# A transformer block on one core: the order of the first requests, and eight row slots in the head

## The chip, the cores and the metric

The kernel runs on 1 core of one Trainium2 chip. The metric is the device time of one execution in microseconds (us). TensorE multiplies, VectorE (DVE), ScalarE (ACT) and GpSimd (POOL) do the elementwise work, and SyncE (SP) issues nearly all transfers between HBM and SBUF. Each engine takes its instructions in the order in which they were written for it and waits on semaphores.

## What is computed

The reference is one transformer block in float32, on x of 1024 rows by 1024 columns:

```python
for l in range(DEPTH):                                   # DEPTH = 1
    x = x + _hybrid_mixer(_rms_norm(x, norm1_g[l]), w_in[l], ...)
    x = x + _memory_xattn(_rms_norm(x, norm2_g[l]), mem, ...)
    x = x + _sq_relu_mlp(_rms_norm(x, norm3_g[l]), w_ff_in[l], w_ff_out[l])
```

The mixer begins with one projection, whose columns are split into the inputs of two attention branches (a top-k one, and one with compressed, selected and windowed keys):

```python
proj = h @ w_in
c_q, c_kv, k_idx, w_idx, q_nsa, kv_nsa, g_nsa = jnp.split(proj, splits, axis=-1)
```

The change touches only how this projection starts: `_rms_norm(x, norm1_g)`, and the product of the first 512 rows with columns 968 to 1224 of `w_in`, which hold the keys and values that are compressed in blocks of 32 positions.

## The kernel before

The 1024 rows are eight tiles of 128, in two parts of four (`PARTS`, L27). `project` (L371) does the projection of one part. Part 0 is the **head** of the program and runs alone; part 1 and all later dense work run beside the attention of earlier tiles (`together`, L113), and the last dense work stands at the end.

In the head each tile of x is loaded (L378), squared and summed on ScalarE (L288), scaled by its inverse root and by the gain norm1_g on VectorE (L290), turned by eight transposes on TensorE (L277), and split into a rounded high half xh on ScalarE (L238) and a low half xl, the rest, on VectorE (L239). Weights are loaded in groups of 256 rows (`load_w`, L254) into a ring of four raw slots and split likewise into whi on ScalarE (L247) and wlo on GpSimd or VectorE (L252). A product in `gemm` (L303) loads the four groups of a chunk of columns and then goes over the four tiles; every tile is 8 k-steps of three matmuls (xh by whi, xh by wlo, xl by whi; L221), summed in one PSUM buffer and then consumed (`consume`, L408). The first chunk, columns 968 to 1224, is copied by a relu-tagged tile (L434), transposed (L437) and stored as the compression's input. The chunks that follow use the same four row tiles.

Ahead of all that, the constants are asked for where `build` comes to them: the identity (L226), cos and sin (L349, L350), the q gains (L352 to L354), the xq gain (L358), the masks (L359, L361, through two slots of the row ring and a cast, L204), and the position encodings of the compression (`pe_stack`, L1143), which are transposed on TensorE and copied on GpSimd (L486, L487) to the end of the compression's input. In `project`, after the tiles, come the gains of the compressed queries and keys and a table (L387 to L390), and seven rows of key gains (L397). Most of these are one row sent to all 128 partitions.

Row tiles, the gain norm1_g, the normalized rows and the masks' raw form share one ring of SBUF slots, tag `x4` (L38), five slots in the head.

The order on each engine is not the order of the lines. The program is built with `schedule_with_timeline_sim` (L82): a scheduler sets the order of each engine's instructions from its own model of their times, with the written order as a guide. Every request of SyncE also waits for the landing of the request eight places before it, since eight semaphores are used in turn.

Of the kernel before, what the change touches and what calls it, by code (L numbers as in the profile page):

```python
# [9 lines left out]
F32 = mybir.dt.float32  # L10
# [7 lines left out]
ALU = mybir.AluOpType  # L18
# [4 lines left out]
P = 128  # L23
L = 1024
DM = 1024
NT = L // P
PARTS = ((0, 4), (4, 4))  # L27
# [6 lines left out]
KG = 2  # L34
NS = 4
G = 2
RINGS = {
    "p1": {"x4": 5, "st": 2, "relu": 4, "wraw": 4, "whi": 6, "wlo": 6, "c8": 4, "c4": 2, "kraw": 5, "pc": 2},  # L38
    "p2": {"x4": 3, "st": 1, "relu": 2, "whi": 4, "wlo": 4, "c8": 3, "c4": 1, "kraw": 4, "pc": 2},
    "dn": {"b4": 4, "h": 8, "relu": 2, "wraw": 2, "whi": 4, "wlo": 4},  # L40
    "res": {"b4": 4},
# [45 lines left out]
def drain(gen):  # L87
    for _ in gen:
        pass
# [80 lines left out]
def build(nc, tc, I, C, out):  # L170
    v, s, g, te = nc.vector, nc.scalar, nc.gpsimd, nc.tensor
    ctx = ExitStack()
    W = {n: I[n][0] for n in I}
# [14 lines left out]
    def ring(pool, tag, shape, dt=F32):  # L188
        n = RINGS[pool.name if isinstance(pool.name, str) else "dn"][tag]
        return pool.tile(shape, dt, tag=tag, name=tag, bufs=n)  # L190

    def row(ap):
        return ap[None, :]

    def const(name, shape, pool=cst):
        t = pool.tile(shape, F32, tag=name, name=name)
        nc.sync.dma_start(t, C[name])
        return t

    def const16(name, shape):  # L200
        t = at.tile(shape, BF16, tag=name, name=name)
        f = ring(p1, "x4", shape)
        nc.sync.dma_start(f, C[name])
        v.tensor_copy(t, f)  # L204
        return t

    def bcast(name, src, w):
        t = cst.tile([P, w], F32, tag=name, name=name)
        nc.sync.dma_start(t, src.to_broadcast([P, w]))
        return t  # L210

    def swap(x):
        return halves(x)[..., ::-1, :]

    def halves(x):
        if len(x.shape) == 2:
            return x.rearrange("p (j i) -> p j i", j=2)
        return x.rearrange("p h (j i) -> p h j i", j=2)

    def mm(o, a, b, start, stop):  # L220
        te.matmul(o, a, b, start=start, stop=stop)  # L221

    def small(pool, tag, w, dt=F32, bufs=2, p=P):
        return pool.tile([p, w], dt, tag=tag, name=tag, bufs=bufs)

    ident = const("c_ident", [P, P])  # L226
    mhalf = cst.tile([P, 1], F32, tag="mhalf", name="mhalf")
    v.memset(mhalf, -0.5)
# [25 lines left out]
    def load_w(pool, shape, *srcs):  # L254
        raw = ring(pool, "wraw", shape)
        for dst, src in srcs:
            nc.sync.dma_start(dst(raw), src)
        hi, lo = ring(pool, "whi", shape, F32R), ring(pool, "wlo", shape, F32R)
        split_w(raw, hi, lo)
        return hi, lo  # L260
# [3 lines left out]
    def load_whole(pool, shape, *srcs):  # L264
        wholes["i"] += 1
        raw = ring(pool, ("whi", "wlo")[wholes["i"] % 2], shape)
        for dst, src in srcs:
            nc.sync.dma_start(dst(raw), src)
        return [raw]
# [30 lines left out]
            v.scalar_tensor_tensor(xn, x_t[:, c:c + 512], r[:, 0:1], gb[c // 512], op0=ALU.mult, op1=ALU.mult)  # L300
            to_T(pool, xn, [x[:, c // P:c // P + 4] for x in xs], 4)

    def gemm(pool, xs, nk, nt, wsrc, chunks, consume):  # L303

        for ci, parts in enumerate(chunks):
            w = sum(n for _, n in parts)
            gr = []
            for k0 in range(0, nk, KG):
                kn = min(KG, nk - k0)
                srcs, o = [], 0  # L310
                for c0, n in parts:
                    srcs.append((lambda r, o=o, n=n: r[:, :, o:o + n],
                                 wsrc[k0 * P:(k0 + kn) * P, c0:c0 + n].rearrange("(k p) n -> p k n", p=P)))
                    o += n
                ws = load_w(pool, [P, kn, w], *srcs) if len(xs) == 2 else load_whole(pool, [P, kn, w], *srcs)
                gr += [[x[:, k, :] for x in ws] for k in range(kn)]
            for t in range(nt):
                pt = pst(TAGS[pool.name][0], [P, w])
                for k in range(nk):
                    if len(xs) == 1:  # L320
                        mm(pt, xs[0](t, k), gr[k][0], k == 0, k == nk - 1)
                        continue
                    wh, wl = gr[k]
                    xh, xl = xs[0](t, k), xs[1](t, k)
                    mm(pt, xh, wh, k == 0, False)
                    mm(pt, xh, wl, False, False)
                    mm(pt, xl, wh, False, k == nk - 1)
                consume(ci, t, pt)
                yield nk * (5 - len(xs)) * w / 2400.0

    def xT(pool, nt, whole=False):

        parts = [pool.tile([P, DM // P, nt * P], F32 if whole else F32R, tag="x" + n, name="x" + n)
                 for n in ("h" if whole else "hl")]
        return (parts, [lambda t, k, x=x: x[:, k, t * P:(t + 1) * P] for x in parts],
                lambda t: [x[:, :, t * P:(t + 1) * P] for x in parts])
# [9 lines left out]
            nc.sync.dma_start(gb, row(src[i * 512:(i + 1) * 512]).to_broadcast([P, 512]))  # L346
        return gs

    cos = const("c_cos", [P, NT, 32], at)  # L349
    sin = const("c_sin", [P, NT, 64], at)  # L350
    qg = at.tile([P, 3, 64], F32, tag="qg", name="qg")
    nc.sync.dma_start(qg[:, 0, :], row(W["dsa_qn_g"]).to_broadcast([P, 64]))  # L352
    nc.sync.dma_start(qg[:, 1, :], row(W["nsa_qn_g"]).to_broadcast([P, 64]))
    nc.sync.dma_start(qg[:, 2, :], W["nsa_kn_g"][0:1].to_broadcast([P, 64]))  # L354
    v.tensor_scalar(qg[:, 0:2, :], qg[:, 0:2, :], -1.0, None, op0=ALU.mult)
    qgs = at.tile([P, 3, 64], F32, tag="qgs", name="qgs")
    v.tensor_copy(halves(qgs), swap(qg))
    xqg = bcast("xqg", row(W["xq_norm_g"]), 128)  # L358
    masks = const16("c_masks", [P, 640])  # L359
    window, causal = masks[:, 0:512], masks[:, 128:640]  # L360
    cmask = const16("c_cmask", [P, NT, 64])  # L361
    qraw = [[[dr.tile([P, n, 256], F32, tag=f"q{k}{t}{c}", name=f"q{k}{t}{c}") for c in range(2)] for t, n in PARTS]
            for k in range(3)]
    oT_dr = [[dr.tile([P, P], F32, tag=f"o{t}{c}", name=f"o{t}{c}") for c in range(8)] for t in range(NT)]
# [3 lines left out]
    xo_dr = [dr.tile([P, 512], F32, tag=f"xo{t}", name=f"xo{t}") for t in range(NT)]  # L368


    def project(pool, part, pe, st):  # L371
        t0, nt = PARTS[part]
        gb1 = gain(pool, W["norm1_g"])
        whole = part > 0
        _, xf, xt_of = xT(pool, nt, whole)
        for t in range(nt):
            x_t = ring(pool, "x4", [P, DM])
            nc.sync.dma_start(x_t, I["x"][0, (t0 + t) * P:(t0 + t + 1) * P, :])  # L378
            norm_T(pool, x_t, gb1, xt_of(t))
            yield 1.0  # L380
        cq = [ring(pool, "c8", [P, nt, 2, P], F32 if whole else F32R) for _ in xf]
        ckv = [ring(pool, "c4", [P, nt, P], F32 if whole else F32R) for _ in xf]
        kraw = [ring(pool, "kraw", [P, 6, 64]) for t in range(nt)]
        KT = []
        pc = ring(pool, "pc", [P, 512])
# [59 lines left out]
                s.activation(kraw[t][:, 2 * b:2 * b + 2, :], pt[:, :128].rearrange("p (a d) -> p a d", d=64), AF.Copy)  # L445
                split_ps(pt[:, 128:256].rearrange("p (a d) -> p a d", d=64), V[:, T, :, 0, :], V[:, T, :, 1, :])

        def w_in(chunks, first):
            return gemm(pool, xf, DM // P, nt, W["w_in"], chunks,
                        lambda ci, t, pt: consume(ci + first, t, pt))  # L450

        def consume_kv(ci, t, pt):
            s.activation(kraw[t][:, DSA, :], pt[:, :64], AF.Copy)
# [30 lines left out]
        for kv in range(0 if part else 2):  # L484
            p3 = pe[:, kv, :].rearrange("p (a l) -> p a l", a=2)
            g.tensor_copy(KT[kv][0:64, :, nt * P:], p3[0:64])  # L486
            g.tensor_copy(KT[kv][64:128, :, nt * P:nt * P + 15], p3[64:128, :, 1:])  # L487
        yield from w_in([[(968, 256)]], 4)
        yield from w_in([[(0, 256)], [(256, 200), (1736, 24)]], 0)
        pair_ = (w_in([[(1224, 256)], [(1480, 256)]], 5), compress(pool, part, KT, pe, st, ctab))  # L490
        yield from (alternate if part == 0 else chain)(*pair_)
# [3 lines left out]
        for k, name in ((0, "w_dsa_uq"), (2, "w_idx_q")):  # L495
            yield from gemm(pool, [lambda t, k, c=c: c[:, t, k, :] for c in cq], 2, nt,
                            W[name], [[(0, 256)], [(256, 256)]],
                            lambda ci, t, pt, k=k: stage_q(k, ci, t, pt))
# [644 lines left out]
    def pe_stack():  # L1143
        pe = p1.tile([P, 2, 32], F32, tag="pe", name="pe")
        pe2 = ring(p1, "relu", [P, 2, 2, 64])
        for j in range(2):
            nc.sync.dma_start(pe2[0:32, :, j, :], W["nsa_cmp_pe"].rearrange("k l d -> l k d"))
        pp = pst("M", [P, 2, 32])
        for kv in range(2):
            te.transpose(pp[:, kv, :], pe2[0:32, kv, :, :].rearrange("p a d -> p (a d)"), ident[0:32, 0:32])  # L1150
        s.activation(pe, pp, AF.Copy)
        return pe
# [13 lines left out]
    }  # L1166
    for kv in range(2):
        v.memset(st["cT"][kv], 0.0)
    pe = pe_stack()
    plan["w"] = PLAN_HEAD  # L1170
    drain(project(p1, 0, pe, st))
    plan["w"] = PLAN_MAIN
    p1_psum.__exit__(None, None, None)
    p1_pool.__exit__(None, None, None)
# [6 lines left out]
    def fill():  # L1181
        for part in range(1, len(PARTS)):
            with tc.tile_pool(name="p2", bufs=1, reuse_waits="tile") as p2:
                yield from project(p2, part, pe, st)
            projected.append(part)
        dn = dn_pool.__enter__()
        yield from memory(dn)
        yield 1, PACES[1]
        yield from between(dn, 0, 2, {}, False)
        yield 3, PACES[2]  # L1190
        x2s = {}
        yield from between(dn, 2, 2, x2s, True)
        yield 3, PACES[3]
        yield from mlp(dn, 0, 4, x2s)
        yield 5, PACES[4]
        yield from between(dn, 4, 2, {}, False)
# [40 lines left out]
```

## Time and profile before

| what | value |
|---|---|
| time, median of 3 runs | 1802.85 us (1801.54 to 1806.27) |
| time of the profiled execution | 1801.64 us |
| its span in the profile | 1799.6 us |
| mean granted TensorE clock | 0.977 of full |
| DMA moved over the span | 193.80 MB, mean 108 GB/s |

A line of the order in time gives the start and the length in us, the engine, the line of the kernel, the operation, the tile written and the tile read, the shape and how many were merged; the brackets hold the idle time of that engine before it and what ended it. "SPq" is SyncE's issue of a transfer, not its landing; the landing shows as the end of a wait. In the view of stretches each engine has its busy time and, in parentheses, the number of instructions; the last three numbers are the granted clock, the busy share of the DMA engines, and GB/s.

### The profile page before, as it was taken

The page shows a single profiled execution, that of the slowest core. Times are in us where ns is not written, and L with a number is a line of the kernel's source. Part 1 is how long each engine was busy: PE and PEld are TensorE (multiplying, and loading weights), DVE is VectorE, ACT ScalarE, POOL GpSimd, SP SyncE. Part 2 cuts the span into 40 slices and gives each one's busy share as a digit, 9 for nine tenths or more (in the row PEclk, how much of TensorE's full clock was granted, in tenths as well). Part 3 has the DMA queues.
Part 4 walks back from the last instruction along what each step waited for, and adds up shares of the span by engine and source line. Part 5 has one row for each costly group of instructions (what it writes and reads, how often), then busy time and mean ns, then how long its engine had stood idle before and what let it go on. Part 6 is the DMA issues. An engine that isn't in the chain of part 4 may idle for free.

```text
span 1799.6 us, 28055 instructions
## 1 busy us (share of the span) xinstructions
PE 1696.2 (94%) x9326; PEld 1457.3 (81%) x9326; DVE 951.0 (53%) x2381; ACT 1080.4 (60%) x2703; POOL 892.6 (50%) x1025
## 2 busy tenths in 40 slices
PE   5987999899989999999998999999999889999998
PEld 5986888688878777788886888887988878888887
DVE  4555757665873776365654555646524552222223
ACT  4444659797688579856896557994412543333333
POOL 2356647463551355568576576662211444444445
PEclk9997999999999999999999999999989899999999
DMA  6235221366336321222222122225375642333333
GB/s 193 74 119 150 71 76 58 109 197 177 99 107 192 98 63 42 70 71 79 61 67 83 55 71 67 67 75 187 108 245 158 209 118 84 96 94 98 96 118 107
DMA packets 176977, 193.80 MB, mean 108 GB/s; under 512 B 25664, under 2 KB 144192, under 8 KB 176832
## 3 DMA queue, kind: packets, MB, share of 16 engines
q1 hardware_dynamic: 168896, 181.52, 33.2%
q0 software_dynamic: 7936, 10.49, 2.2%
q8 instruction: 74, 1.21, 0.3%
q14 instruction: 71, 0.58, 0.1%
HBM read 170.98 MB, written 20.97 MB: 107 GB/s over the span
## 4 chain that ended last, share of the span: by engine, by line
PE 67%; DVE 9%; POOL 7%; ACT 5%; issue 5%; DMA 5%; SPq 1%; POOLq 0%; ACTq 0%; DVEq 0%
PE psD L221 48%; PE psS L221 8%; PE psPV L221 5%; PE psPT L698 4%; POOL wlo L252 3%; DMA wraw<-in_w_ff_in_dram 1%; PE psM L277 1%; ACT dmask L639 1%; DVE pl L239 1%; DVE S L681 1%; PE psPT L585 1%; ACT S L683 1%; ACT ph L238 1%; DMA qin<-q 1%; ACT whi L247 1%
## 5 line engine op out<-in xcount | busy, mean ns | idle before, releaser
L252 POOL TENSOR_TENSOR wlo<-wraw,whi 128x512 fp32r<-128x512 f32 (+1 forms) x225 | 309.5, 1380 | 266.7 <-ACT whi L247 263.0
L221 PE MATMUL psD<-whi,h 128*128 128x512 f32 x1024 | 340.7, 401 | 9.7 <-DVE b L1126 5.4
L247 ACT ACTIVATE whi<-wraw 128x512 fp32r<-128x512 f32 x321 | 200.7, 628 | 216.7 <-PE psD L221 156.4
L221 PEld LDWEIGHTS psD<-whi,h 128*128 128x128 f32 x1024 | 193.0, 190 | 55.2 <-DVE b L1126 8.8
L221 PE MATMUL psD<-xh,whi 128*128 128x512 f32 (+1 forms) x576 | 212.1, 372 | 1.2 <-ACT xh L238 0.8
L221 PE MATMUL psD<-xh,wlo 128*128 128x512 f32 (+1 forms) x576 | 212.9, 370 | 0.2 <-POOL wlo L252 0.2
L221 PE MATMUL psD<-xl,whi 128*128 128x512 f32 (+1 forms) x576 | 212.1, 370 | 0.0
L221 PE MATMUL psD<-wlo,h 128*128 128x512 f32 x512 | 203.2, 399 | 1.1 <-POOL wlo L252 1.1
L221 PE MATMUL psD<-whi,xh 128*128 128x256 f32 (+1 forms) x704 | 191.7, 353 | 4.3 <-ACT whi L247 3.2
L221 PE MATMUL psD<-wlo,xh 128*128 128x256 f32 (+1 forms) x704 | 191.3, 354 | 1.3 <-DMA wlo<-in_w_in_dram 0.7
L239 DVE TENSOR_TENSOR pl<-psPT,ph 128x512 fp32r<-128x512 f32 (+1 forms) x232 | 142.0, 620 | 80.1 <-ACT ph L238 77.4
L683 ACT ACTIVATE S<-S,mn 128x128 f32<-128x128 f32 (+7 forms) x192 | 142.6, 744 | 38.5 <-DVE mn L681 36.9
L688 POOL TENSOR_SCALAR S<-S,sums,gi 128x640 f32<-128x640 f32 (+7 forms) x128 | 107.0, 846 | 113.7 <-DVE sums L686 101.8
L252 DVE TENSOR_TENSOR wlo<-wraw,whi 128x512 fp32r<-128x512 f32 (+1 forms) x96 | 83.8, 873 | 148.8 <-ACT whi L247 148.5
L238 ACT ACTIVATE ph<-psPT 128x512 fp32r<-128x512 f32 (+1 forms) x232 | 122.7, 539 | 63.2 <-PE psPT L698 59.0
L221 PEld LDWEIGHTS psD<-wlo,xh 128*128 128x128 f32 x704 | 133.3, 194 | 13.4 <-ACT relu L416 1.2
L221 PEld LDWEIGHTS psD<-whi,xh 128*128 128x128 f32 x704 | 130.7, 194 | 14.2 <-ACT whi L247 3.6
L698 PE MATMUL psPT<-c_ident,S 128*128 128x128 f32 x816 | 131.4, 277 | 3.0 <-POOL S L688 1.6
L221 PEld LDWEIGHTS psD<-xh,whi 128*128 128x128 f32 x576 | 108.8, 189 | 19.3 <-ACT xh L238 1.6
L221 PEld LDWEIGHTS psD<-xh,wlo 128*128 128x128 f32 x576 | 109.0, 189 | 17.6 <-POOL wlo L252 0.9
L221 PEld LDWEIGHTS psD<-xl,whi 128*128 128x128 f32 x576 | 108.8, 189 | 17.1
L221 PE MATMUL psS<-K,qh 128*128 128x384 f32 (+3 forms) x288 | 112.7, 395 | 8.6 <-DVE mn L681 4.0
(282 smaller groups left out, 3863.7 us busy)
## 6 DMA issues: line engine op xcount, KB each, us to landing
wraw<-in_w_ff_in_dram SPq DMA_DIRECT2D x40, 512.0 KB, 4.0
wraw<-in_w_ff_out_dram SPq DMA_DIRECT2D x40, 512.0 KB, 3.9
wraw<-in_w_ff_in_dram SPq DMA_DIRECT2D x64, 256.0 KB, 2.7
wraw<-in_w_ff_out_dram SPq DMA_DIRECT2D x64, 256.0 KB, 2.7
whi<-in_w_out_dram SPq DMA_DIRECT2D x32, 256.0 KB, 3.6
wlo<-in_w_out_dram SPq DMA_DIRECT2D x32, 256.0 KB, 3.7
wraw<-in_w_in_dram SPq DMA_DIRECT2D x24, 256.0 KB, 3.7
q<-st SPq DMA_DIRECT2D x12, 512.0 KB, 2.6
```

Of the source, the lines that this page charges most:

```text
L221: te.matmul(o, a, b, start=start, stop=stop)
L238: s.activation(hi, src, AF.Copy)
L239: v.tensor_tensor(lo, src, hi, op=ALU.subtract)
L247: s.activation(hi, raw, AF.Copy)
L252: (v if l == "v" else g).tensor_tensor(lo, raw, hi, op=ALU.subtract)
L277: te.transpose(pt[:, j, :], x_t[:, (c + j) * P:(c + j + 1) * P], ident)
L585: te.transpose(p2[:, h, :], qd[:, h, :, :].rearrange("p b d -> p (b d)"), ident)
L639: s.activation(mask, src, AF.Sign, bias=c, accum_out=over)
L681: v.tensor_tensor_reduce(out=dst, in0=sp, in1=m, scale=1.0, scalar=mn[:, 0:1] if i else 3e38, op0=ALU.add, op1=ALU.min, accum_out=low)
L683: s.activation(S, S, AF.Exp, bias=low, scale=-1.0, accum_out=sums[:, hh:hh + 1])
L688: g.tensor_scalar(Ss[hh], Ss[hh], sums[:, hh:hh + 1], 1.0 if gate is None else gate[:, hh:hh + 1], op0=ALU.mult, op1=ALU.mult)
L698: te.transpose(p2[:, j, hh, :], S[:, (c + j) * P:(c + j + 1) * P], ident)
```

## The change

The ring `x4` of the head has eight slots in place of five. The first tile of x is asked for ahead of the identity. `project` for part 0 now asks, in this order, for the gain and then alternately for a weight group of the first chunk and a tile of x, before any tile is normalized; `gemm`'s loading of weights becomes a generator, `weights`, from which the first product takes its four groups as `begun`. After the four norms of part 0, all the constants except the identity are asked for, and the position encodings are stacked; then the rest of `project` runs. The values computed are the same.

In the built program SyncE's first ten requests are x, identity, gain, weights, x, weights, x, weights, x, weights. The 21 that follow are cos, sin, three q gains, the xq gain, the position encodings (two), the gains of the compressed queries and keys, the two halves of the table, one key gain, the two masks, and six more rows of key gains. Then come the second chunk's weights. Before, the same 31 requests stand ahead of those weights.

```diff
-    "p1": {"x4": 5, "st": 2, ...
+    "p1": {"x4": 8, "st": 2, ...
...
+    late = {"x": ring(p1, "x4", [P, DM])}
+    nc.sync.dma_start(late["x"], I["x"][0, 0:P, :])
     ident = const("c_ident", [P, P])
...
+    def weights(pool, xs, nk, wsrc, parts):
+        w = sum(n for _, n in parts)
+        for k0 in range(0, nk, KG):
...
+            ws = load_w(pool, [P, kn, w], *srcs) if len(xs) == 2 else load_whole(pool, [P, kn, w], *srcs)
+            for k in range(kn):
+                yield [x[:, k, :] for x in ws]
+
-    def gemm(pool, xs, nk, nt, wsrc, chunks, consume):
+    def gemm(pool, xs, nk, nt, wsrc, chunks, consume, begun=None):
...
+            gr = begun if ci == 0 and begun else list(weights(pool, xs, nk, wsrc, parts))
...
+    ahead = {0: late["x"]}
+    def project(pool, part, late, st):
         gb1 = gain(pool, W["norm1_g"])
...
+        begun = []
+        if not whole:
+            ws = weights(pool, xf, DM // P, W["w_in"], [(968, 256)])
+            for t in range(1, nt):
+                begun += [next(ws) for _ in range(KG)]
+                ahead[t] = ring(pool, "x4", [P, DM])
+                nc.sync.dma_start(ahead[t], I["x"][0, t * P:(t + 1) * P, :])
+            begun += list(ws)
         for t in range(nt):
-            x_t = ring(pool, "x4", [P, DM])
-            nc.sync.dma_start(x_t, I["x"][0, (t0 + t) * P:(t0 + t + 1) * P, :])
+            x_t = ahead.pop(t0 + t, None)
+            if x_t is None:
+                x_t = ring(pool, "x4", [P, DM])
+                nc.sync.dma_start(x_t, I["x"][0, (t0 + t) * P:(t0 + t + 1) * P, :])
             norm_T(pool, x_t, gb1, xt_of(t))
             yield 1.0
+        pe = late["pe"]
...
-    pe = pe_stack()
     plan["w"] = PLAN_HEAD
-    drain(project(p1, 0, pe, st))
+    head = project(p1, 0, late, st)
+    for _ in range(PARTS[0][1]):
+        next(head)
+    cos = const("c_cos", [P, NT, 32], at)
+    sin = const("c_sin", [P, NT, 64], at)
...
+    masks = const16("c_masks", [P, 640])
+    window, causal = masks[:, 0:512], masks[:, 128:640]
+    cmask = const16("c_cmask", [P, NT, 64])
+    late["pe"] = pe_stack()
+    drain(head)
```

More of the change, by code (lines that the diff above doesn't have):

```diff
@@ L37 @@
 RINGS = {
-    "p1": {"x4": 5, "st": 2, "relu": 4, "wraw": 4, "whi": 6, "wlo": 6, "c8": 4, "c4": 2, "kraw": 5, "pc": 2},
+    "p1": {"x4": 8, "st": 2, "relu": 4, "wraw": 4, "whi": 6, "wlo": 6, "c8": 4, "c4": 2, "kraw": 5, "pc": 2},
     "p2": {"x4": 3, "st": 1, "relu": 2, "whi": 4, "wlo": 4, "c8": 3, "c4": 1, "kraw": 4, "pc": 2},
@@ L301, in norm_T2 @@
             to_T(pool, xn, [x[:, c // P:c // P + 4] for x in xs], 4)
-    def gemm(pool, xs, nk, nt, wsrc, chunks, consume):
+    def weights(pool, xs, nk, wsrc, parts):
+        w = sum(n for _, n in parts)
+        for k0 in range(0, nk, KG):
+            kn = min(KG, nk - k0)
+            srcs, o = [], 0
+            for c0, n in parts:
+                srcs.append((lambda r, o=o, n=n: r[:, :, o:o + n],
+                             wsrc[k0 * P:(k0 + kn) * P, c0:c0 + n].rearrange("(k p) n -> p k n", p=P)))
+                o += n
+            ws = load_w(pool, [P, kn, w], *srcs) if len(xs) == 2 else load_whole(pool, [P, kn, w], *srcs)
+            for k in range(kn):
+                yield [x[:, k, :] for x in ws]
+    def gemm(pool, xs, nk, nt, wsrc, chunks, consume, begun=None):
         for ci, parts in enumerate(chunks):
             w = sum(n for _, n in parts)
[L307 to L316, printed above, removed]
+            gr = begun if ci == 0 and begun else list(weights(pool, xs, nk, wsrc, parts))
             for t in range(nt):
@@ L347, in gain2 @@
         return gs
[L349 to L361, printed above, removed]
     qraw = [[[dr.tile([P, n, 256], F32, tag=f"q{k}{t}{c}", name=f"q{k}{t}{c}") for c in range(2)] for t, n in PARTS]
@@ L368, in build @@
     xo_dr = [dr.tile([P, 512], F32, tag=f"xo{t}", name=f"xo{t}") for t in range(NT)]
-    def project(pool, part, pe, st):
+    ahead = {0: late["x"]}
+    def project(pool, part, late, st):
         t0, nt = PARTS[part]
@@ L446, in consume, with w_in @@
                 split_ps(pt[:, 128:256].rearrange("p (a d) -> p a d", d=64), V[:, T, :, 0, :], V[:, T, :, 1, :])
-        def w_in(chunks, first):
+        def w_in(chunks, first, begun=None):
             return gemm(pool, xf, DM // P, nt, W["w_in"], chunks,
-                        lambda ci, t, pt: consume(ci + first, t, pt))
+                        lambda ci, t, pt: consume(ci + first, t, pt), begun)
         def consume_kv(ci, t, pt):
@@ L487, in project @@
             g.tensor_copy(KT[kv][64:128, :, nt * P:nt * P + 15], p3[64:128, :, 1:])
-        yield from w_in([[(968, 256)]], 4)
+        yield from w_in([[(968, 256)]], 4, begun)
         yield from w_in([[(0, 256)], [(256, 200), (1736, 24)]], 0)
@@ L1168, in build @@
         v.memset(st["cT"][kv], 0.0)
-    pe = pe_stack()
     plan["w"] = PLAN_HEAD
-    drain(project(p1, 0, pe, st))
+    head = project(p1, 0, late, st)
[3 more added lines that the diff above has]
+    sin = const("c_sin", [P, NT, 64], at)
+    qg = at.tile([P, 3, 64], F32, tag="qg", name="qg")
+    nc.sync.dma_start(qg[:, 0, :], row(W["dsa_qn_g"]).to_broadcast([P, 64]))
+    nc.sync.dma_start(qg[:, 1, :], row(W["nsa_qn_g"]).to_broadcast([P, 64]))
+    nc.sync.dma_start(qg[:, 2, :], W["nsa_kn_g"][0:1].to_broadcast([P, 64]))
+    v.tensor_scalar(qg[:, 0:2, :], qg[:, 0:2, :], -1.0, None, op0=ALU.mult)
+    qgs = at.tile([P, 3, 64], F32, tag="qgs", name="qgs")
+    v.tensor_copy(halves(qgs), swap(qg))
+    xqg = bcast("xqg", row(W["xq_norm_g"]), 128)
+    masks = const16("c_masks", [P, 640])
[3 more added lines that the diff above has]
+    drain(head)
     plan["w"] = PLAN_MAIN
@@ L1183, in fill @@
             with tc.tile_pool(name="p2", bufs=1, reuse_waits="tile") as p2:
-                yield from project(p2, part, pe, st)
+                yield from project(p2, part, late, st)
             projected.append(part)
```

## The prediction

> **What bounds the kernel now.** I read the page first, for the share of each engine and the chain that ended last; then busy time in stretches, to find where TensorE is not busy; then the order in time of the first 41 us, and the DMA issues of that stretch.
>
> The page of the kernel before, span, engines and the chain by engine:
> ```profile
> span 1799.6 us, 28055 instructions
> PE 1696.2 (94%) x9326; PEld 1457.3 (81%) x9326; DVE 951.0 (53%) x2381; ACT 1080.4 (60%) x2703; POOL 892.6 (50%) x1025
> PE 67%; DVE 9%; POOL 7%; ACT 5%; issue 5%; DMA 5%; SPq 1%; POOLq 0%; ACTq 0%; DVEq 0%
> ```
> TensorE bounds the whole, so a change of the head is worth what it moves TensorE's stream. Busy time in stretches of it:
> ```profile
> 0.00:24.00 24.00, 3.87 (x17) 3.36 (x18) 6.46 (x15) 6.10 (x11) 3.40 (x11) 1.00 0.65 202
> 24.00:41.00 17.00, 16.84 (x131) 16.55 (x130) 13.15 (x19) 12.83 (x26) 5.89 (x6) 1.00 0.71 185
> 41.00:125.00 84.00, 81.81 (x709) 80.83 (x709) 46.31 (x114) 39.94 (x125) 41.14 (x40) 1.00 0.31 91
> 125.00:150.00 25.00, 12.82 (x73) 11.02 (x71) 5.50 (x16) 7.56 (x17) 6.56 (x9) 0.68 0.66 217
> 200.00:1799.00 1599.00, 1533.05 (x8126) 1303.63 (x8126) 846.51 (x2085) 983.90 (x2417) 803.73 (x900) 0.98 0.35 105
> ```
> The first number after the stretch and its length is TensorE's busy time. In the first 24 us it is idle for 24 - 3.87 = 20.1 us; from 24 to 125 it is busy 98.7 of 101. So the head is a wait, then a full stream, and the wait is what the change can take away. Its steps, in order of time (start, length, engine and line):
> ```profile
> 0.73 0.38 SPq L197 DMA_DIRECT2D c_ident<-in_c_ident_dram  x1
> 4.96 2.23 SPq L1147 DMA_DIRECT2D relu<-in_nsa_cmp_pe_dram  x2
> 7.77 0.35 SPq L378 DMA_DIRECT2D x<-in_x_dram  x1
> 13.83 1.06 ACT L288 ACTIVATE x<-x 128x1024 f32<-128x1024 f32 x1 [1.95 <-DMA x<-in_x_dram]
> 15.97 1.28 DVE L290 SCALAR_TENSOR_TENSOR x<-x,nr,x 128x1024 f32<-128x1024 f32 x1 [0.74 <-POOL nr L234]
> 16.40 1.72 SPq L257 DMA_DIRECT2D wraw<-in_w_in_dram  x2
> 17.31 1.97 PE L277 MATMUL psM<-c_ident,x 128*128 128x128 f32 x8 [5.69 <-DVE x L290]
> 21.80 1.40 ACT L247 ACTIVATE whi<-wraw 128x512 fp32r<-128x512 f32 x2 [0.93 <-DMA wraw<-in_w_in_dram]
> 22.48 0.58 PE L221 MATMUL psD<-whi,xh 128*128 128x256 f32 x1 [3.21 <-ACT whi L247]
> 23.82 4.03 SPq L257 DMA_DIRECT2D wraw<-in_w_in_dram  x3
> 24.42 0.56 PE L221 MATMUL psD<-wlo,xh 128*128 128x256 f32 x1
> 27.34 0.41 PE L221 MATMUL psD<-whi,xh 128*128 128x256 f32 x1
> 27.56 0.41 PE L221 MATMUL psD<-whi,xl 128*128 128x256 f32 x1
> 28.36 0.28 PE L221 MATMUL psD<-wlo,xh 128*128 128x256 f32 x1
> 28.47 0.28 PE L221 MATMUL psD<-whi,xl 128*128 128x256 f32 x1
> 29.06 0.68 DVE L239 TENSOR_TENSOR xl<-psM,xh 128x512 fp32r<-128x512 f32 x1
> 30.13 1.09 ACT L238 ACTIVATE xh<-psM 128x512 fp32r<-128x512 f32 x2 [0.42 <-PE psM L277]
> 40.91 0.60 ACT L434 ACTIVATE relu<-psD 128x512 f32<-128x512 f32 x1
> ```
> The first rows of x are asked for at 7.77 and land at 13.83; the first weights land at 21.80; the first real product starts at 22.48. The second weights are asked for at 23.82. The last row marks the end of the first product (the relu of its fourth tile), so TensorE's second product begins at about 40.9. That moment is my yardstick: from there to the end of the head both programs have TensorE's instructions in the same order.
>
> **The change part by part.** Nothing is removed or added: 31 requests stand ahead of the second product's weights in both programs, the same 31. They change places: x, ident, gain, weights, x, weights and so on are 1 to 10, then come the 21 for constants. What they cost is read from the issues of the first 40 us (KB each, median us to landing; the first row is GB/s in slices of 1 us):
> ```profile
> GB/s 0 27 203 244 25 18 24 98 344 287 352 320 370 234 47 19 173 326 193 177 202 396 384 372 224 318 330 212 76 199 161 247 212 224 243 186 210 62 174 67
> wraw<-in_w_in_dram SPq DMA_DIRECT2D x8, 256.0 KB, 4.6
> x<-in_c_masks_dram SPq DMA_DIRECT2D x1, 320.0 KB, 6.1
> c_sin<-in_c_sin_dram SPq DMA_DIRECT2D x1, 256.0 KB, 2.8
> c_ident<-in_c_ident_dram SPq DMA_DIRECT2D x1, 64.0 KB, 1.9
> xqg<-in_xq_norm_g_dram SPq DMA_DIRECT2D x1, 64.0 KB, 5.7
> ```
> *Gain at the start.* x is now request 1, at 0.73. The 64 KB of ident took 1.9 us, the 256 KB of c_sin 2.8; 512 KB at the 318 GB/s of slices 8 to 13 are 1.6 us behind that 1.9, so x lands at about 4.3 in place of 13.83. The same 3.48 us (13.83 to 17.31) bring the first transposes to 7.8. The first weights, fourth in the line (1.38 MB, 4.3 us at that rate, from about 2), land near 6.5, so they no longer hold the first product; ScalarE, which also squares the second tile, hands over the first xh at about 11. That is 11 us earlier than 22.48.
>
> *What is late next.* Here I follow the order in which the changed program's queues stand. Each request waits for the landing of the one eight places before it. x3 and w3 (9 and 10) land at 2 + 3.74 MB / 318 GB/s = 13.8, about 14. The small broadcasts wait behind these; requests 17 and 18 (nsa_cmp_pe, 2.23 us for both) wait for x3 and w3, so five more requests at 0.4 to 0.5 bring c_masks (24) to about 18.5, by the spacing that SyncE shows (0.73 to 4.96 for the first nine). Its slot in the ring is free by then (it waits for the first normalized tile's transposes). With its own 6.1 us it lands at 24.6; with the 1.9 of ident, the shortest landing here, at 20.4. I take 23.5, nearer to its own row, with 20.5 and 26.5 (one such short landing more than 24.6) for the ends.
>
> Three queues are held by that landing. VectorE has the cast of c_masks ahead of the xl of the third and fourth tiles. SyncE asks for the second product's first weights (request 32) only when c_masks, eight places before, is there. ScalarE has the whi of those weights ahead of the fourth tile's xh. So the first product's last tile now waits for the second product's weights. From 23.5: weights 5.4 us (16.40 to 21.80, the w of before that also stood behind small broadcasts; 4.6 is the median) to 28.9; whi and xh (0.7 + 0.55) 30.2; the second whi, a relu (0.60) and the second xh, 32.0; xl 0.68, 32.7; then the last 12 matmuls at 0.11 (28.36 to 28.47) and four transposes, 1.8 in all: 34.5. The second product thus begins at 34.5 in place of 40.9, **6.4 us earlier**: of the 11 us won at the start, some 4.6 are lost because the constants stand where the idle time was filled. The ends 20.5 and 26.5 of the landing give 9.4 and 3.4.
>
> A rule that bears on this: the Trainium skill, page DMA: Bandwidth & Descriptors, section Rules for kernel authors, says that under 64 KB a transfer pays mostly overhead. The slices from 4 to 7 us (25, 18, 24 GB/s) agree. By it the whole head could be bound by its requests; that is the second rival below, which is priced from the slices alone.
>
> *A slow restart.* From 24.42 to 27.56 the matmuls followed each other at 0.22 us (27.34 to 27.56), from 28 on at 0.11, at a granted clock of 1.00 in both stretches. Were the stream that restarts after c_masks as slow for as long, it would lose half of 3.1 us, 1.6. I take nothing, because that stream still waits for the fourth tile's xh afterwards, and keep 1.6 for the range. The Trainium skill, page TensorE: Matmul & The Clock Gate, Part 1, says that an idle window of about 3.4 us puts TensorE back to half clock and a busy one releases it. The spacing in the trace agrees; by that rule the slow restart would come in this change, and the sum would be 4.8 in place of 6.4.
>
> *Covers.* The chain of work (start, length) has the first use of cos, and the order in time has the copies of the position stack:
> ```profile
> 99.27 1.40 POOL relu L468
> ```
> ```profile
> 11.94 0.20 POOL L486 COPY c<-pe 64x32 f32<-64x32 f32 x1 [11.50 <-ACT pe L1151]
> ```
> Cos, at 99, and the masks, in attention, land by 30 and so cost nothing. The position stack (L1150) moves from the front into the third tile's product and into TensorE's queue; nsa_cmp_pe, asked for at about 15, lands by 21 at 5.7 us like xqg, before c_masks, so it costs nothing; if that cover goes, everything behind it on TensorE waits. Four copies of the stack now stand on GpSimd ahead of the third lo half of the second product: 0.8 us, under the 1.4 us of that product's first 12 matmuls. Eight row slots are what lets four rows, the gain and three normalized rows stand at once; the first ten requests wait for no slot.
>
> *Passing it on.* From 41 to 125 TensorE idles 2.2 us, so the shift passes through. At 125 the q stores hold SyncE until the last of them; the part-1 requests behind wait, in the changed program, for earlier events than that. So the dip of 125 to 150 moves along rigidly. Behind 200 the instructions are the same but a scheduler has set many of them in another order: a cost I can't read from any row. I bound it by TensorE's idle time there, 1599 - 1533.05 = 66 us: a tenth of it either way, 6.6 us, as one end and the other, and take zero, since nothing in the order favours a side.
>
> Sum: the profiled execution took 1801.64 us (span 1799.6 and 2.0 around it), 1.2 below the median of the runs, 1802.85. 1801.64 - 6.4 = **1795.2**; I give 1795.
>
> **Rivals.**
> 1. *The start's gain survives better.* If c_masks lands at 20.5 or before, or the weights take 4.6, the second product begins 9 to 10 us earlier. For it: the wire moved 318 GB/s and more when it had large transfers, and all large ones now stand in a row. Against: ten small ones precede c_masks. Time: 1801.64 - 10 = 1791 to 1792.
> 2. *The constants only change places; the change doesn't do what it says.* Four broadcasts filled the 3.5 us from 4 to 7.5, so one takes 0.9. The ten small requests between w3 (14) and c_masks then take 9 us and its own and other bytes 1.6: 24.6; the six behind it plus c_cmask and the weights take 5.4 + 1.6, so the weights land at about 32 and the second product starts at 37.6, 3.3 us earlier. Time: 1798, or 1800 with the slow restart. For: request 32 left at 23.82 before, behind the same 31. Against: from 8 to 14 us smalls and large ones shared the wire without loss.
> 3. *Slower.* The new order of the attention part (200 to 1799) costs TensorE more than the head gives. Place: waits of TensorE between interleaved products and attention tiles. Price: with a fifth more than the 66 us of idle there, 13.2 - 6.4 = 6.8 us, 1808. It decides once the added idle is above 6.4, a tenth. For: the order differs in most of that part. Against: the engines' work is the same, and the last part of the order is unchanged.
>
> **How the numbers follow.** Forecast (4.5 to 9 us at the end, about 1793 to 1797): 0.46. First rival, with a lucky order: 0.18. Second: 0.22. Third: 0.14. A change of 0.3%, 5.4 us, is about what a measurement of this kernel can tell from none. Of the forecast's cases some 0.36 are beyond it, with the first rival 0.54 faster; the rest, the second rival and a bit of the third are the same, 0.34; slower 0.12. The range runs from 1786 (first rival's 9.4 plus the order's 6.6) to 1805 (most of the second rival with the order against it).
>
> **What would show it.** First transposes at about 7.8 and first product at 11, not 17.3 and 22.5; c_masks' cast at 23 to 25 on VectorE with xl right behind it; TensorE idle for some us before 30; the relu of the fourth tile at about 34. If that relu stands at 31 or less, the first rival holds; at 37 or more, the second. If it stands at 34 and the time is not 1795, the order of the later part did it: TensorE's idle time behind 200 would then differ from 66. Wrong I am too if the position stack's landing holds TensorE in the third tile, which a wait at that line would show.

## The result, and the profile after

The changed kernel is slower: 1815.60 us median of 4 runs (1814.04 to 1817.51) against 1803.44 us of the kernel before in the same session (1801.54 to 1806.27), a ratio of 1.0067 with a 95% interval of 1.0049 to 1.0084. The forecast was 1795. The profiled execution took 1814.04 us.

The page after, span, engines and the chain by engine:
```profile
span 1812.3 us, 28011 instructions
PE 1699.8 (94%) x9326; PEld 1460.8 (81%) x9326; DVE 947.0 (52%) x2381; ACT 1080.0 (60%) x2703; POOL 886.7 (49%) x1025
PE 50%; DMA 3%; POOL 3%; DVE 3%; issue 2%; ACT 2%; SPq 0%; POOLq 0%; ACTq 0%; DVEq 0%
```
TensorE has the same number of instructions and is busy 3.6 us more, in a span that is 12.7 us longer: most of the loss is time in which it waits. Busy time in the stretches of the prediction, after:
```profile
0.00:24.00 24.00, 12.44 (x77) 11.54 (x77) 11.64 (x22) 11.60 (x20) 4.99 (x10) 1.00 0.66 221
24.00:41.00 17.00, 13.42 (x98) 13.04 (x99) 7.90 (x15) 8.13 (x19) 4.54 (x7) 0.90 0.88 190
41.00:125.00 84.00, 82.85 (x700) 82.06 (x700) 45.75 (x116) 40.27 (x126) 38.62 (x37) 1.00 0.28 88
125.00:150.00 25.00, 12.11 (x65) 10.00 (x63) 6.04 (x12) 6.84 (x16) 7.53 (x13) 0.73 0.68 220
200.00:1799.00 1599.00, 1522.44 (x8074) 1295.40 (x8074) 838.36 (x2073) 981.78 (x2409) 796.13 (x896) 0.98 0.34 104
```
Three things are to be seen. The first 24 us hold 12.44 us of TensorE work in place of 3.87, as intended. The next 17 hold 13.42 in place of 16.84, at a granted clock of 0.90: of the 8.6 us won, 3.4 are given back at once. And behind 200 us TensorE idles 1599 - 1522.44 = 76.6 us in place of 66.0. That stretch ends before the longer span does; over the whole span TensorE idles 1812.3 - 1699.8 = 112.5 us (103.4 before), and 29.2 of it lie in the first 150 us (34.7 before). So the head idles 5.5 us less, and the part behind 150 us 83.3 in place of 68.7: **14.6 us more**.

The head in order of time, after:
```profile
4.39 1.06 ACT L290 ACTIVATE x<-x 128x1024 f32<-128x1024 f32 x1 [2.39 <-DMA x<-in_x_dram]
7.64 1.28 DVE L292 SCALAR_TENSOR_TENSOR x<-x,nr,x 128x1024 f32<-128x1024 f32 x1 [1.91 <-DMA x<-in_norm_g_dram]
8.98 1.97 PE L279 MATMUL psM<-c_ident,x 128*128 128x128 f32 x8 [8.98 <-DVE x L292]
12.11 0.58 PE L221 MATMUL psD<-whi,xh 128*128 128x256 f32 x1 [1.16 <-ACT xh L240]
23.33 0.49 DVE L204 CAST c_masks<-x 128x640 bf16<-128x640 f32 x1 [2.57 <-DMA x<-in_c_masks_dram]
23.38 2.23 SPq L259 DMA_DIRECT2D wraw<-in_w_in_dram  x4
29.03 0.63 ACT L249 ACTIVATE whi<-wraw 128x512 fp32r<-128x512 f32 x1 [8.00 <-DMA wraw<-in_w_in_dram]
30.17 0.69 DVE L241 TENSOR_TENSOR xl<-psM,xh 128x512 fp32r<-128x512 f32 x1 [4.68 <-ACT xh L240]
30.92 1.12 PE L444 MATMUL psM<-c_ident,relu 128*128 128x128 f32 x4 [3.10 <-DVE xl L241]
37.57 0.58 ACT L441 ACTIVATE relu<-psD 128x512 f32<-128x512 f32 x1
```
Read from below: the fourth tile's relu stands at 37.57 (40.91 before). TensorE waited 3.10 us for an xl, VectorE 4.68 for the xh of it, and ScalarE 8.00 us for the second product's weights, whose whi is queued ahead of that xh. These weights were asked for at 23.38, when c_masks had landed.

How much of this arrives at the end of the head shows where part 1 begins, with the request for its norm's gain. Before, and after:
```profile
131.91 0.38 SPq L340 DMA_DIRECT2D x<-in_norm_g_dram  x1
```
```profile
129.51 0.38 SPq L347 DMA_DIRECT2D x<-in_norm_g_dram  x1
```
The head gives 2.4 us in this execution. Up to here the kernel is ahead, and in the end it is 12 behind: some 15 us, the added idle time, are lost behind the head, where the same instructions run in another order.

### The profile page after: what moved, and what is told of

It reads as the page before. It is cut to its first block, busy times and chain, and to the rows that moved or that the text cites. A ratio compares the mean times of both kernels' runs of the same rounds, so it can differ in the third digit from the quotient of the medians.

```text
span 1812.3 us, 28011 instructions
## 1 busy us (share of the span) xinstructions
PE 1699.8 (94%) x9326; PEld 1460.8 (81%) x9326; DVE 947.0 (52%) x2381; ACT 1080.0 (60%) x2703; POOL 886.7 (49%) x1025
## 4 chain that ended last, share of the span: by engine, by line
PE 50%; DMA 3%; POOL 3%; DVE 3%; issue 2%; ACT 2%; SPq 0%; POOLq 0%; ACTq 0%; DVEq 0%
PE psD L221 37%; PE psS L221 7%; PE psPV L221 3%; PE psPT L705 3%; POOL wlo L254 1%; DMA wraw<-in_w_ff_in_dram 1%; DMA wraw<-in_w_ff_out_dram 1%; ACT whi L249 0%; POOL h L1040 0%; DMA whi<-in_w_out_dram 0%; PE psM L279 0%; DVE b L1133 0%; ACT dmask L646 0%; POOL S L695 0%; DMA b<-x 0%
## 5 line engine op out<-in xcount | busy, mean ns | idle before, releaser
L254 DVE TENSOR_TENSOR wlo<-wraw,whi 128x512 fp32r<-128x512 f32 (+1 forms) x96 | 78.1, 815 | 138.9 <-ACT whi L249 138.6
L221 PEld LDWEIGHTS psD<-xl,whi 128*128 128x128 f32 x576 | 108.6, 189 | 17.5
```

Of the source, the lines that this page charges most:

```text
L254: (v if l == "v" else g).tensor_tensor(lo, raw, hi, op=ALU.subtract)
```

## The theories

**Theory 1**: the new head gives a few us, and the order that the scheduler gives to the part behind it costs some 15. **Rival 2**: the new head itself costs it, by its slots or by what it leaves behind. **Rival 3**, for the means used: links that fix an order cost time of their own. For the head itself: **1a**, ScalarE's whi of late weights holds the first product's last tile; **1b**, VectorE's cast of the masks does.

In the experiments with a fixed order each engine's instructions behind the head are chained, each to the one before it on its own engine. So nothing waits for another engine that didn't before; only the scheduler's choice is gone. The list of the order stands at the top of those kernels, which moves their line numbers up by some 140 to 170.

One thing is needed to read the times. The 29 runs of the kernel before in the session of e1 to e4 go from 1796.24 to 1807.58 us, and their mean granted clock from 0.983 (1798.14) to 0.974 (1807.58). So differences of 2 or 3 us are read from the traces, not from the times. The ratio given with a run is the one on record; it isn't the quotient of the two medians.

## The experiments

**e1, the changed head with the old order.**
```diff
+    made = len(nc.cur_bb.bb.instructions)
     plan["w"] = PLAN_MAIN
...
+    pin(tc, nc, made)
     ctx.close()
...
+def pin(tc, nc, made):
...
+            if prev is not None:
+                tc.add_manual_dep(mine[e][at], prev.name,
+                                  mybir.DependencyInfo(mybir.DependencyClass.NoSync, mybir.DependencyReason.DATA),
+                                  reason="pin")
```


> The changed kernel's head as it is; every instruction behind the head set on its engine in the order of the kernel before, by added order links that make nothing wait on another engine. Theory 1 (the head yields 2.4 to 3.3 us and the new order of the later part costs some 15): 1803.4 - 2.4 to 3.3 = 1800 to 1801, faster than before by 0.13 to 0.18%, and TensorE's idle time behind 200 us back from 77 to about 66 us. Rival 2 (the head itself, by its slots or by what it leaves behind, costs the time later): 1815, as the changed kernel. Rival 3 (the links cost time of their own): above 1803, with waits in the later part at other places than in the kernel before.

Measured: 1800.44 us median of 12 runs (1794.41 to 1803.28) against 1802.92; ratio 0.9997 (0.9981 to 1.0012). Stretches of it:
```profile
575.00:680.00 105.00, 97.47 (x562) 82.48 (x561) 78.72 (x238) 70.74 (x180) 43.43 (x56) 0.96 0.30 91
200.00:1799.00 1599.00, 1533.88 (x8111) 1304.96 (x8109) 844.76 (x2077) 982.34 (x2409) 800.79 (x894) 0.98 0.34 105
```
By tile names, the instructions of every engine behind 205 us stand in the trace in the order of the kernel before, as they were meant to. TensorE's idle time behind 200 us is 65.1, that of before (66.0) within a us, and the 105 us of the first line are busy as before (below). The 15 us are gone with the order alone, the head being the changed one: rival 2 falls, and rival 3 too. Whether the kernel is now faster than before can't be said from the interval; at a granted clock of 0.977 the medians are 1800.44 (4 runs) and 1804.28 (5 runs). Its head gave more than in the changed kernel's profile:
```profile
30.40 0.65 PE L589 MATMUL psM<-c_ident,relu 128*128 128x128 f32 x4 [2.42 <-DVE xl L386]
127.47 0.38 SPq L492 DMA_DIRECT2D x<-in_norm_g_dram  x1
```
Part 1's gain is asked for at 127.47, 4.4 us earlier than before. The four transposes that took 1.12 us behind an idle time of 3.10 take 0.65 behind one of 2.42. The changed kernel in slices of that time:
```profile
28.00:30.00 2.00, 0.00 (x0) 0.00 (x0) 0.00 (x0) 0.97 (x2) 0.27 (x1) 1.00 1.20 280
30.00:32.00 2.00, 1.08 (x5) 1.08 (x6) 1.52 (x3) 1.85 (x5) 1.00 (x1) 0.70 1.22 160
32.00:34.00 2.00, 2.00 (x12) 2.00 (x11) 1.16 (x3) 1.24 (x4) 0.82 (x4) 0.50 0.79 147
34.00:36.00 2.00, 2.00 (x18) 2.00 (x18) 0.67 (x2) 1.48 (x3) 0.43 (x1) 0.95 0.99 219
```
The clock (the first of the last three numbers) falls short by 2 x (0.30 + 0.50 + 0.05) = 1.7 us of full speed: the slow restart. In e1 it is 1.00 in all of them.

**e2, the head of before with the changed kernel's order.** The same links, with the other order, in the kernel before.

> The counterpart: the head of the kernel before, with everything behind it in the order that the changed kernel has. Theory 1: 1815.6 + 2.4 to 3.3 = 1818 to 1819, slower than before by 0.8%, though nothing of the change is in its head. Rival 2: 1803, as before.

Measured: 1820.40 us median of 6 runs (1818.32 to 1826.74); ratio 1.0124 (1.0100 to 1.0148). Nothing of the change is in this head, the instructions behind 205 us stand in the changed kernel's order, and the kernel is 17.5 us slower, some more than expected. The order costs that with either head. Where it lies shows in one stretch; e2, then before, after, and e8 (below):
```profile
575.00:680.00 105.00, 90.56 (x510) 77.71 (x508) 69.12 (x215) 63.17 (x159) 36.62 (x50) 0.92 0.26 80
```
```profile
575.00:680.00 105.00, 96.87 (x570) 81.75 (x569) 79.50 (x241) 71.54 (x181) 43.90 (x56) 0.98 0.30 90
```
```profile
575.00:680.00 105.00, 88.61 (x514) 75.75 (x513) 75.90 (x230) 65.89 (x166) 41.15 (x54) 0.95 0.25 76
```
```profile
575.00:680.00 105.00, 88.27 (x518) 75.57 (x517) 76.56 (x230) 65.07 (x161) 42.18 (x55) 0.95 0.20 62
```
With the old order, before and e1, TensorE is busy 96.9 and 97.5 of these 105 us; with the new one, after, e2 and (up to 690 us the same order) e8, 88.6, 90.6 and 88.3. Idle time behind 150 us, worked out as above for the one profiled execution of each kernel (span less TensorE's busy time, less the idle time of the first 150 us):

| order of the later part | kernel: idle us behind 150 us |
|---|---|
| that of before | before 68.7, e1 70.8, e3 69.3, e4 68.3, e5 68.7, e6 70.0 |
| the changed kernel's | after 83.3, e2 84.1 |
| another, by the scheduler | e7 72.8 (for the most part that of before), e8 85.5 (up to 690 us the changed kernel's) |

The head doesn't matter in this table, the order does. What it waits for there, after (us in total, times, longest):
```profile
PE psM L279 <- DMA relu<-xo: 3.4, 1, 3.4
PE psM L279 <- ACT xh L283: 2.1, 2, 1.4
PE psM L279 <- DVE xl L241: 2.0, 1, 2.0
PE psM L279 <- DVE h L241: 1.6, 1, 1.6
```
The largest in this stretch is a way through memory: a tile is stored to xo, read back as relu (request on SyncE) and transposed. After, and before:
```profile
631.40 0.33 SPq L994 DMA_DIRECT2D relu<-xo  x1
634.22 0.63 PE L279 MATMUL psM<-c_ident,relu 128*128 128x128 f32 x4 [3.36 <-DMA relu<-xo]
```
```profile
632.51 0.33 SPq L987 DMA_DIRECT2D relu<-xo  x1
636.38 0.63 PE L277 MATMUL psM<-c_ident,relu 128*128 128x128 f32 x4 [0.46 <-DMA relu<-xo]
```
From request to transposes it is 2.8 us after and 3.9 us before: the transfer is no slower. But before, TensorE's queue holds other work between, and it waits 0.46; after, the transposes stand right behind too little work, and it waits 3.36. Such a wait is paid a second time:
```profile
630.00:640.00 10.00, 6.64 (x35) 5.88 (x35) 4.48 (x15) 4.94 (x13) 2.87 (x3) 0.83 0.33 97
```
In the changed kernel's 10 us around it the clock is 0.83 (1.00 before), another 1.7 us. The stretch of 105 us holds 8.3 of the 14.6 us of added idle time; the 425 us ahead of it give 1.5 back, and what lies behind it costs 7.8. There the changed order has single waits that are longer still. But so has the old order, at other places. After, and before:
```profile
993.69 0.80 PE L221 MATMUL psD<-whi,h 128*128 128x512 f32 x1 [3.60 <-DVE b L901]
1484.00 0.50 PE L221 MATMUL psD<-whi,h 128*128 128x512 f32 x1 [3.89 <-DVE b L1133]
```
```profile
523.29 1.12 PE L277 MATMUL psM<-c_ident,relu 128*128 128x128 f32 x4 [3.94 <-DMA relu<-xo]
1469.95 1.09 PE L277 MATMUL psM<-c_ident,relu 128*128 128x128 f32 x4 [3.80 <-DVE xl L239]
```
In the first two TensorE waits for VectorE's adds into b; the third is the way through xo again, here bare in the old order. So the 14.6 us are a balance of waits gained and lost, and no single chain is shown to be their cause.

**e3, the slots alone.**
```diff
-    "p1": {"x4": 5, "st": 2, ...
+    "p1": {"x4": 8, "st": 2, ...
```


> The kernel before with eight row slots in the head in place of five and nothing else; its later order is that of the kernel before. Theory 1: the slots alone do nothing, 1803 (within 1.5 us of before). Rival 2, if the slots are what costs: slower by some of the 12 us. The x rows could be asked for sooner, but x is the fifth row tile after the constants and stands behind them in the queue, so no gain either.

Measured: 1803.74 us median of 12 runs (1799.26 to 1807.23); ratio 1.0015 (1.0000 to 1.0029). The slots bring and cost nothing that matters.

**e4, the head mended**, with the old order.
```diff
-    "p1": {"x4": 8, ..., "wraw": 4, "whi": 6, "wlo": 6, ...
+    "p1": {"x4": 6, ..., "wraw": 8, "whi": 7, "wlo": 7, ...
...
             begun += list(ws)
+            second = list(weights(pool, xf, DM // P, W["w_in"], [(0, 256)]))
...
-        yield from w_in([[(0, 256)], [(256, 200), (1736, 24)]], 0)
+        yield from w_in([[(0, 256)]], 0, None if whole else second)
+        if not whole:
+            yield "masks"
+        yield from w_in([[(256, 200), (1736, 24)]], 1)
...
+    while next(head) != "masks":
+        pass
     masks = const16("c_masks", [P, 640])
```
(The gains `pc` and `kg`, cos, sin and xqg also move behind the first product's code, the position stack ahead of the q gains, and the casts of the masks are linked behind the second product's last VectorE instruction.)

> The idea of the change carried on, with the later order of the kernel before: the weights of the second product are asked for right behind those of the first (eight raw slots, seven for each half), the first product is issued ahead of the gains, and the masks are asked for and cast behind it, so that VectorE, ScalarE and SyncE have nothing of the constants ahead of the first product's last tile. If what cost the head's gain was c_masks on those three queues (Theory 1), the relu of the fourth tile comes at 27 to 31 us instead of 37.6, and the time is 1803.4 - 7 to 11 = 1792 to 1796. If the small requests or ScalarE's conversions set the head whatever the order (rival), the relu stays at 35 to 38 and the time at 1799 to 1801.

Measured: 1795.99 us median of 12 runs (1792.86 to 1798.97); ratio 0.9971 (0.9957 to 0.9986). This version beats both kernels. Its stretch and its boundary:
```profile
24.00:41.00 17.00, 16.93 (x140) 16.35 (x139) 9.19 (x21) 9.12 (x25) 4.22 (x8) 1.00 0.87 216
```
```profile
125.40 0.37 SPq L495 DMA_DIRECT2D x<-in_norm_g_dram  x1
```
TensorE has hardly any idle time left between 24 and 41, part 1 begins 6.5 us earlier than before, and the time falls by 6.9 between the medians (2.5 to 7.8 by the interval of the ratio): what the head gives does arrive at the end, as far as the times can tell, if the order behind it stands. The expected mark failed: the fourth tile's relu stood at 35.23, where the rival had put it, since on ScalarE it is now queued behind the whi of the third product's weights. TensorE had gone on to the second product: by count, the last of the first product's 96 matmuls starts at 32.2, and at 40.5 in the kernel before. An instruction of one engine is a poor mark for another's progress.

**e5 and e6, the two halves of the mending**, one run each. e5 has the ring sizes and `second` of e4's diff; e6 has its masks.

> One half of the mended head, the later order as before: only the second product's weights asked for ahead (behind the first product's), the constants where the changed kernel has them. The first look at the old-order kernel had TensorE idle 2.4 us at 28 us, in front of the first product's last tile, and asked for part 1's gain at 127.47; the mended head had no such idle time and asked at 125.40. If what held the last tile was ScalarE's whi of weights that came late (Theory 1a), the idle time is gone here: under 0.5 us between 24 and 32 us, gain asked for at 125 to 126. If it was VectorE's cast of c_masks (Theory 1b), which stands here later still (2.7 us more, for 1 MB more at 390 GB/s ahead of it), the idle time is as long or longer and the gain is asked for at 127 or after.

> The other half: only the two masks asked for behind the second product's weights, these where they were. Theory 1a: the weights of the second product are asked for some 1 to 2 us sooner but ScalarE still has their whi ahead of the fourth tile's xh, so TensorE still waits 1 to 2.5 us there; gain of part 1 at 126 to 127.5. Theory 1b: no wait of over 0.5 us there, gain at 125 to 126.

Measured, e5:
```profile
29.41 0.43 DVE L349 CAST c_cmask<-x 128x512 bf16<-128x512 f32 x1 [2.78 <-DMA x<-in_c_cmask_dram]
30.49 0.66 PE L590 MATMUL psM<-c_ident,relu 128*128 128x128 f32 x4 [1.72 <-DVE xl L386]
126.79 0.37 SPq L492 DMA_DIRECT2D x<-in_norm_g_dram  x1
```
and e6:
```profile
22.49 2.58 SPq L404 DMA_DIRECT2D wraw<-in_w_in_dram  x4
27.94 0.63 ACT L394 ACTIVATE whi<-wraw 128x512 fp32r<-128x512 f32 x1 [7.06 <-DMA wraw<-in_w_in_dram]
32.20 1.12 PE L589 MATMUL psM<-c_ident,relu 128*128 128x128 f32 x4 [5.41 <-DVE xl L386]
131.45 0.37 SPq L492 DMA_DIRECT2D x<-in_norm_g_dram  x1
```
Neither met its numbers. In e5 the wait is shorter (1.72 us, from 2.42) but not gone: with the whi out of the way, VectorE's cast of the other mask, c_cmask, is next in line. In e6 the weights are asked for only 0.4 us sooner than in e1 (22.49; 22.89 there), because other small requests stand ahead of them still; ScalarE has two whi ahead of the last xh now, TensorE waits 5.41 us and restarts slowly (the transposes take 1.12), and the head gives 0.5 us. So 1a holds in its direction: ScalarE is the first hold, VectorE the second, and by the boundary moving the masks alone is worse than leaving them. The times of these single runs, 1795.06 and 1796.47, lie within what the clock alone moves, so nothing is read from them.

**e7, another order by a small move**: in the kernel before only the position stack goes behind the first four norms.
```diff
-    pe = pe_stack()
...
+    for _ in range(PARTS[0][1]):
+        next(head)
+    late["pe"] = pe_stack()
+    drain(head)
```


> The kernel before with one thing moved: the position stack is asked for and transposed behind the first four rows' norms. No constant and no weight is asked for otherwise, so by the head alone it is 1803 (within 2 us). But the scheduler gives the later part an order that is neither that of before nor that of the changed kernel. Theory 1 (the order of the later part is a draw, worth many us): the time is off 1803 by several us in either direction, and what it is off by stands as TensorE idle time behind 200 us. Rival (only what the changed head leaves behind makes the order bad): 1803 within 2 us.

Measured: 1804.34 us median of 10 runs (1797.12 to 1808.84); ratio 0.9997 (0.9979 to 1.0014). Here the rival's number came.
```profile
575.00:680.00 105.00, 95.60 (x551) 81.17 (x550) 75.86 (x232) 69.66 (x174) 43.76 (x56) 0.97 0.29 91
```
In the stretch where the changed kernel's order loses 8.3 us, this one loses 1.3, and behind 150 us 4.1 in all. But it is a weak test: by tile names, TensorE's matmuls stand here in the same order as in the kernel before from 574 to 676 us, the stretch shown, and from 1076 us to the end. So a small change of the order can cost nothing that the times show; whether a wholly new order can isn't shown. The rival's reason, that the changed head makes the order bad, falls with e2.

**e8, the mended head with the scheduler's own order**: e4 without the links of the later part.

> The mended head with the later part left to the scheduler, as the change itself does it. The head gives 6.5 us at the gain of part 1. Theory 1: the time is 1796 plus what this draw of the order costs or gives, off 1796 by several us; the changed kernel's order shares its first third, so I expect 1800 to 1812. Rival: 1796 within 2 us.

Measured: 1809.53 us median of 10 runs (1805.73 to 1812.38) against 1804.56 in its session; ratio 1.0031 (1.0018 to 1.0044). The same head ends 6.9 us below the kernel before with the old order and 5.0 above it with the free one, each in its own session: 12 us between them. Its lines stand with e2's: 88.27 busy in the 105 us, 85.5 us idle behind 150. By tile names, TensorE's matmuls stand in the changed kernel's order up to 690 us, over a third of the program, and the kernel loses in the same place.

## Why the prediction was wrong

**Passing it on** is the step that failed. It took zero for the new order of the part behind 200 us, "since nothing in the order favours a side", and bounded it at 6.6 us, a tenth of TensorE's idle time. The runs show 15 us with the changed head (e1 against the changed kernel), 17.5 with the old one (e2), 12 with the mended one (e8 against e4). The bound was drawn from the wrong quantity: the waits that an order holds off aren't limited by those that are left. An example is the way through xo at 632 us: 3.9 us long, it was covered by other work but for 0.46, and the changed order has 3.36 us of it bare. Which chains make up the whole of the 14.6 us, and why this order is the worse one, stays open. The third rival was right in place and sign, and its size came out by luck: it priced a fifth more of 66 us, 13.2, where 14.6 are measured, but the fifth was read from no row, and with the 6.4 of the head it gave 1808, not 1814. 1801.64 - 2.4 + 14.6 = 1813.8 is the profiled execution's 1814.04 within 0.3. Its chance, 0.14, was low for an order that was seen to differ in most of the part. The sentence of the same step on the head's end held in e4, where the order stayed and 6.5 us at 125 became 6.9 between the medians; e1's 4.4 at 127 are 2.5 between the medians and can't be told from nothing by the ratio.

**Gain at the start** was nearly right: x at 4.39 (4.3 forecast), the first product at 12.11 (11). The transposes came at 8.98 in place of 7.8, because the norm's gain landed later than x, for which VectorE waited 1.91 us.

**What is late next** had the chain right: c_masks at 23.33 (23.5), ScalarE's whi at 29.03 (28.9). The first agrees partly by luck: c_masks was asked for at 19.27, 0.8 later than forecast, and took 4.0 us to land, not the 5.0 assumed. The mis-sized term is what stands behind it on TensorE: "the last 12 matmuls ... and four transposes, 1.8". TensorE resumes at 30.92, sooner than the 32.7 of the sum, but with 28 matmuls and 12 transposes of the first product still to do, which took until about 37. It stood at the transposes of the first tile's relu, which take a buffer of PSUM that the fourth tile's xl frees; I had counted only what reads that xl. The head thus gives 4.4 us (e1) in place of 6.4.

**A slow restart**, priced at 1.6 and taken as nothing, came in the changed kernel and cost 1.7 by the clock; 2.4 us were left at the boundary. The reason given for nothing, that the stream waits afterwards anyway, didn't hold: behind 30.92 it was full. The Trainium skill, page TensorE: Matmul & The Clock Gate, Part 1, states that an idle window of about 3.4 us brings half clock; the head's rows agree in kind, with full clock behind 1.72 and 2.42 us of waiting and half clock behind 3.10 and 5.41, but later waits of about 2 us brought half clock too (last section).

**Covers** held: no wait at the position stack, none for cos or the masks in attention. The second rival gave 37.6 for the fourth tile, and it came at 37.57, but by luck and not by its mechanism: it had c_masks at 24.6 and the weights at 32.

## What to carry to other kernels

Where a scheduler orders a long program, an edit of its first 40 us is also an edit of all that follows: compare the order behind the edit, and if it changed, measure the edit with the old order fixed and the new order under the old head, before anything is said of the edit itself. The idle time that is left is no bound for a changed order: 6.6 us, a tenth of it, was taken here, and 14.6 came. The length of the chains that are covered now may be the better bound; that wasn't tested. And in a head of strict queues, ask for each moved request which instruction on which engine waits for it and what stands behind that one, down to the buffers it frees.

## What the runs showed of the hardware

- In the head, behind 28 us, TensorE restarted at full clock behind waits of 1.72 and 2.42 us and at half clock behind 3.10 and 5.41; the restart behind 3.10 cost 1.7 us. The length of a wait doesn't decide it alone: in the changed kernel a wait of 2.10 us ends at 334.53 and one of 1.97 at 675.96, and the clock behind them is a half:
```profile
334.53:337.50 2.97, 2.97 (x7) 2.43 (x8) 0.30 (x3) 1.97 (x7) 0.00 (x0) 0.51 0.15 50
675.96:678.00 2.04, 2.04 (x8) 1.75 (x9) 2.04 (x9) 1.98 (x5) 1.72 (x3) 0.50 0.00 0
```
- At the start of a run the clock column is no guide: in the kernel before, 12 matmuls start from 26 to 28 us and 19 from 28 to 30, and it shows 1.00 for both. The prediction's "granted clock of 1.00 in both stretches" rests on it.
- From run to run the same kernel is granted a mean clock of 0.974 to 0.983, and its time spreads over 11 us, nearly as much as the change makes. In e1, 2.5 us between the medians are 3.8 us at the same clock of 0.977.
